# A tuned RMS-norm kernel rewritten as hardware loops with hand-made semaphores

## The chip, the cores and the metric

One NeuronCore of a Trainium2 chip runs the kernel. The metric is device time in microseconds (us) of one execution. All runs quoted are in the fast state, with a granted clock of 1.0 (TensorE's, as the profile gives it), so times can be compared directly. The profile's span is about 2 us shorter than the measured time (162.0 against 164.03 us for the kernel before).

Engine names in the profile: DVE is VectorE, ACT is ScalarE, POOL is GpSimd, SP is SyncE, which here only issues transfers. A name with q (ACTq, DVEq, SPq) is that engine's sequencer; in these profiles the waits of an engine on the hand-made semaphores are put down to it.

## The reference, cut to what matters

```python
x: (16, 1024, 512) float32; gamma: (512,) ones; eps: 1e-5
rms = np.sqrt(np.mean(x ** 2, axis=-1, keepdims=True) + eps)
return np.maximum(x / rms * gamma, 0)
```

There are 16384 rows of 512 floats, 33.55 MB in and as much out.

## The kernel before

Each of 128 partitions handles 128 rows, in eight chunks of 16 rows (4.19 MB). Six chunk buffers ("slots") are loaded at once; loads 6 and 7 reuse the first two slots when their stores are done. A chunk is computed in two groups of G = 8 rows:

```python
junk = psum.tile([P, d], F32, name="junk")            # one scratch row
...
for g in range(ngroups):                              # 2 groups a chunk
    a, b = g * G, (g + 1) * G
    for j in range(a, b):
        nc.scalar.activation(out=junk, in_=xt[:, j, :], func=ACTF.Square,
                             accum_out=ss[i][:, j:j + 1])
    nc.scalar.activation(out=rms[i][:, a:b], in_=ss[i][:, a:b],
                         func=ACTF.Sqrt, bias=eps_sb, scale=inv_d)
    nc.vector.tensor_mul(out=xt[:, a:b, :], in0=xt[:, a:b, :], in1=gammaG())
    nc.vector.reciprocal(out=rstd[i][:, a:b], in_=rms[i][:, a:b])
    for j in range(a, b):
        nc.vector.tensor_scalar(out=xt[:, j, :], in0=xt[:, j, :],
            scalar1=rstd[i][:, j:j + 1], scalar2=0.0, op0=ALU.mult, op1=ALU.max)
```

The squares themselves go to `junk` and are never read; only the row sum is used. The framework writes everything out as straight code and places all waits.

Of the kernel before, what the change touches and what calls it, by code (L numbers as in the profile page):

```python
# [1 line left out]

# [4 lines left out]

F32 = mybir.dt.float32
ALU = mybir.AluOpType
ACTF = mybir.ActivationFunctionType  # L10


@with_exitstack
def kernel(
    ctx: ExitStack,
    tc: tile.TileContext,
    x: bass.AP,
    gamma: bass.AP,
    eps: bass.AP,
    out: bass.AP,  # L20
):


    nc = tc.nc
    P = nc.NUM_PARTITIONS

    x2 = x.flatten_outer_dims()
    out2 = out.flatten_outer_dims()
    n, d = x2.shape
    rows = n // P  # L30
    inv_d = 1.0 / d
    xv = x2.rearrange("(c p k) d -> c p k d", p=P, k=16)
    ov = out2.rearrange("(c p k) d -> c p k d", p=P, k=16)

    K = 16
    G = 8
    nchunks = rows // K
    nslots = 6
    ngroups = K // G

    singles = ctx.enter_context(tc.tile_pool(name="singles", bufs=1))
    slots = ctx.enter_context(tc.tile_pool(name="slots", bufs=1))
    small = ctx.enter_context(tc.tile_pool(name="small", bufs=1))
    psum = ctx.enter_context(
        tc.tile_pool(name="psum", bufs=1, space=bass.MemoryType.PSUM))

    ctx.enter_context(tc.manual_schedule())

    gseed = singles.tile([P, d], F32, name="gseed")
    gamma_sb = singles.tile([P, d], F32, name="gamma_sb")  # L50
    eps_sb = singles.tile([P, 1], F32, name="eps_sb")
    junk = psum.tile([P, d], F32, name="junk")
    slot = [slots.tile([P, K, d], F32, name=f"slot{s}") for s in range(nslots)]
    ss = [small.tile([P, K], F32, name=f"ss{i}") for i in range(nchunks)]
    rms = [small.tile([P, K], F32, name=f"rms{i}") for i in range(nchunks)]
    rstd = [small.tile([P, K], F32, name=f"rstd{i}") for i in range(nchunks)]

    def load(i):
        nc.sync.dma_start(out=slot[i % nslots], in_=xv[i])

    def store(i):
        nc.sync.dma_start(out=ov[i], in_=slot[i % nslots])

    def gammaG():
        g = gamma_sb[:]
        return bass.AP(tensor=g.tensor, offset=g.offset,
                       ap=[g.ap[0], [0, G], g.ap[1]])

    def compute(i):
        xt = slot[i % nslots]  # L70
        for g in range(ngroups):
            a, b = g * G, (g + 1) * G
            for j in range(a, b):
                nc.scalar.activation(out=junk, in_=xt[:, j, :], func=ACTF.Square,  # L74
                                     accum_out=ss[i][:, j:j + 1])
            nc.scalar.activation(out=rms[i][:, a:b], in_=ss[i][:, a:b],  # L76
                                 func=ACTF.Sqrt, bias=eps_sb, scale=inv_d)
            nc.vector.tensor_mul(out=xt[:, a:b, :], in0=xt[:, a:b, :], in1=gammaG())  # L78
            nc.vector.reciprocal(out=rstd[i][:, a:b], in_=rms[i][:, a:b])  # L79
            for j in range(a, b):  # L80
                nc.vector.tensor_scalar(  # L81
                    out=xt[:, j, :], in0=xt[:, j, :],
                    scalar1=rstd[i][:, j:j + 1], scalar2=0.0,
                    op0=ALU.mult, op1=ALU.max)

    nc.vector.memset(gseed, 0.0)  # L86
    nc.vector.memset(eps_sb, eps)  # L87
    for q in range(0, P, 32):
        nc.scalar.dma_start(out=gseed[q:q + 1, :], in_=gamma[None, :])

    for i in range(min(nslots, nchunks)):
        load(i)
    nc.vector.stream_shuffle(gamma_sb, gseed, [0] * 32)  # L93
    for i in range(min(nslots, nchunks)):
        compute(i)
    nxt = nslots
    for i in range(nchunks):
        store(i)
        if i >= 1 and nxt < nchunks:
            load(nxt)  # L100
            compute(nxt)
            nxt += 1


# [1 line left out]
_INS = ['x', 'gamma', 'eps']  # L106
_OUTS = [((16, 1024, 512), 'float32')]

_NUMBERS = {'eps': 9.999999747378752e-06}


# [26 lines left out]
```

## Time and profile before

| quantity | value | where it is read |
|---|---|---|
| time | 164.03 us (163.9 to 164.15, 2 runs) | the timed runs |
| bytes moved | 67.11 MB on one queue, 96.9% of 16 engines' span | queue table |
| DVE busy / ACT busy | 124.6 / 98.5 us | busy table |
| a DVE group / an ACT group | 7.74 / 6.24 us | timeline |
| last store issued / span's end | 143.01 / 162.0 us | timeline |

The prediction reads the bound from the slice view. The windows view of the end shows what it means for the last store. Its columns are the window, its length, the busy time of DVE, ACT and POOL with instruction counts, the clock, the DMA share and GB/s.

```profile
140.00:147.00 7.00, 2.98 (x8) 0.00 (x0) 0.00 (x0) 1.00 1.02 440
147.00:152.00 5.00, 0.00 (x0) 0.00 (x0) 0.00 (x0) 1.00 0.99 426
152.00:157.00 5.00, 0.00 (x0) 0.00 (x0) 0.00 (x0) 1.00 1.02 439
157.00:161.00 4.00, 0.00 (x0) 0.00 (x0) 0.00 (x0) 1.00 0.27 115
```

The last store is issued when compute is finished:

```profile
143.01 0.33 SPq L62 DMA_DIRECT2D out_dram<-slot  x1
```

The queue works in the order of issue: the first four loads, issued at 0.73, 1.16, 1.64 and 2.10 us, land at 13.0, 22.8, 32.7 and 42.3.

### The profile page before, as it was taken

Reading aid. Unit: us, or ns where it says so; the run is one execution under the profiler, and the core shown is the slowest. Engines: PE = TensorE matmul, PEld = TensorE weight load, DVE = VectorE, ACT = ScalarE, POOL = GpSimd, SP = SyncE. Lnnn points to the kernel's source line nnn. Section 1 sums busy time; section 2 is a strip of 40 time slices with the busy share of each in tenths; the row PEclk is TensorE's granted clock in tenths of the full one; section 3 lists DMA queues with packets and bytes.
Section 4 is the critical chain, followed back from the end, with each engine's and each line's share of the span. In section 5 each row is a group of like instructions: output and inputs, shape, how many; then the busy total and the mean of one; then the engine's idle time right before and its main releaser. Section 6 shows DMA issues by size and latency. Waiting matters only on the chain.

```text
span 162.0 us, 554 instructions
## 1 busy us (share of the span) xinstructions
DVE 124.6 (77%) x164; ACT 98.5 (61%) x274; POOL 0.2 (0%) x4
## 2 busy tenths in 40 slices
DVE  1001299999999999999999999999999999920000
ACT  2107999999999999999999199901998000000000
POOL 0000000000000000000000000000000000000000
DMA  6999899999999999998999999999999999999990
GB/s 227 421 405 502 388 413 493 390 421 477 396 421 471 396 388 388 461 445 388 463 437 404 453 445 404 453 437 396 461 429 445 429 421 445 429 421 445 437 413 16
DMA packets 2315, 67.14 MB, mean 414 GB/s; under 512 B 260, under 2 KB 260, under 8 KB 264
## 3 DMA queue, kind: packets, MB, share of 16 engines
q1 hardware_dynamic: 2304, 67.11, 96.9%
q14 instruction: 3, 0.02, 0.0%
q10 hardware_dynamic: 8, 0.01, 0.0%
HBM read 33.56 MB, written 33.55 MB: 414 GB/s over the span
## 4 chain that ended last, share of the span: by engine, by line
DVE 74%; DMA 8%; ACT 3%; issue 2%; DVEq 0%
DVE slot L78 43%; DVE slot L81 30%; DMA slot<-in_x_dram 8%; ACT junk L74 3%; DVE rstd L79 1%; DVEq L133 0%
## 5 line engine op out<-in xcount | busy, mean ns | idle before, releaser
L74 ACT ACTIVATE junk<-slot 128x512 f32<-128x512 f32 x128 | 76.8, 600 | 23.0 <-DMA slot<-in_x_dram 19.5
L78 DVE TENSOR_TENSOR slot<-slot,gamma_sb 128x4096 f32<-128x4096 f32 x16 | 70.7, 4418 | 4.2 <-ACT junk L74 4.2
L81 DVE TENSOR_SCALAR slot<-slot,rstd 128x512 f32<-128x512 f32 x128 | 52.1, 481 | 0.6
L74 ACT ACTIVATION_READ_ACCUMULATOR junk<-slot 128x1 f32 x128 | 23.8, 186 | 0.0
L93 DVE LOAD_MASK_SELECT gamma_sb<-gseed x1 | 0.0, 14 | 12.8 <-DMA gseed<-in_gamma_dram 12.8
L76 ACT ACTIVATE rms<-ss,eps_sb 128x8 f32<-128x8 f32 x16 | 4.8, 301 | 0.5
L74 ACT ACT_TABLE_LOAD x1 | 1.3, 1283 | 3.2 <-issue 3.2
L79 DVE RECIPROCAL rstd<-rms 128x8 f32<-128x8 f32 x16 | 3.1, 194 | 0.0
L76 ACT ACT_TABLE_LOAD x1 | 1.3, 1283 | 0.0
L86 DVE MEMSET gseed<- 128x512 f32 x1 | 0.5, 485 | 0.9 <-PEq L119 0.9
L93 DVE STREAM_SHUFFLE gamma_sb<-gseed 128x512 f32<-128x512 f32 x1 | 0.7, 721 | 0.0
L119 POOL MEMSET const-bfloat16-1.0<- 128x1 bf16 x1 | 0.1, 101 | 0.0
L119 POOL MEMSET const-uint8-127<- 128x1 uint8 x1 | 0.1, 101 | 0.0
L119 POOL MEMSET const-float32-0.0<- 128x1 f32 x1 | 0.1, 99 | 0.2 <-issue 0.2
L119 POOL MEMSET const-float32-1.0<- 128x1 f32 x1 | 0.1, 98 | 0.0
L87 DVE MEMSET eps_sb<- 128x1 f32 x1 | 0.1, 59 | 0.0
## 6 DMA issues: line engine op xcount, KB each, us to landing
slot<-in_x_dram SPq DMA_DIRECT2D x8, 4096.0 KB, 30.6
out_dram<-slot SPq DMA_DIRECT2D x8, 4096.0 KB, 35.4
gseed<-in_gamma_dram ACTq DMA_DIRECT2D x4, 2.0 KB
```

Source lines behind the costliest of these rows:

```text
L74: nc.scalar.activation(out=junk, in_=xt[:, j, :], func=ACTF.Square, accum_out=ss[i][:, j:j + 1])
L76: nc.scalar.activation(out=rms[i][:, a:b], in_=ss[i][:, a:b], func=ACTF.Sqrt, bias=eps_sb, scale=inv_d)
L78: nc.vector.tensor_mul(out=xt[:, a:b, :], in0=xt[:, a:b, :], in1=gammaG())
L79: nc.vector.reciprocal(out=rstd[i][:, a:b], in_=rms[i][:, a:b])
L81: nc.vector.tensor_scalar(out=xt[:, j, :], in0=xt[:, j, :], scalar1=rstd[i][:, j:j + 1], scalar2=0.0, op0=ALU.mult, op1=ALU.max)
L86: nc.vector.memset(gseed, 0.0)
L87: nc.vector.memset(eps_sb, eps)
L93: nc.vector.stream_shuffle(gamma_sb, gseed, [0] * 32)
L119: nc = _bacc.Bacc("TRN2", target_bir_lowering=False, num_devices=1)
```

## The change

The intent is a short program: one critical section (a stretch in which the author, not the framework, places the waits) in which ACT and DVE each run a hardware loop over the 16 groups, with register addresses and the author's own semaphores. Transfers keep their order and sizes. On DVE the reciprocal, which waits for ACT's Sqrt, moves ahead of the multiply. The core of the diff:

```diff
-    junk = psum.tile([P, d], F32, name="junk")
+    junk = psum.tile([P, G, d], F32, name="junk")
+    with tc.tile_critical():
...
+        for i in range(nchunks):
+            nc.gpsimd.wait_ge(sem_ld[i], 16)
+            nc.gpsimd.sem_inc(ready, per)
...
+        with nc.scalar.Fori(0, ngroups) as gi:
+            nc.scalar.wait_ge(ready, 1)
+            nc.scalar.sem_inc(ready, -1)
+            base = nc.scalar.snap((gi % (nslots * per)) * G)
+            col = nc.scalar.snap(gi * G)
+            for j in range(G):
+                a = nc.scalar.activation(
+                    out=junk[:, j, :], in_=slots[:, bass.ds(base + j, 1), :],
+                    func=ACTF.Square, accum_out=ss[:, bass.ds(col + j, 1)])
+                if j == G - 1:
+                    a.then_inc(sa, 1)
+            nc.scalar.wait_ge(sa, 1)
+            nc.scalar.sem_inc(sa, -1)
+            nc.scalar.activation(out=rms[:, bass.ds(col, G)], in_=ss[:, bass.ds(col, G)],
+                                 func=ACTF.Sqrt, bias=eps_sb, scale=inv_d).then_inc(sq, 1)
...
+        with nc.vector.Fori(0, ngroups) as gi:
+            nc.vector.wait_ge(sq, 1)
...
+            nc.vector.reciprocal(out=rstd[:, bass.ds(col, G)], in_=rms[:, bass.ds(col, G)])
+            nc.vector.tensor_mul(out=blk, in0=blk, in1=gammaG).then_inc(sv, 1)
+            nc.vector.wait_ge(sv, 1)
+            nc.vector.sem_inc(sv, -1)
... (eight tensor_scalar, the last raising `done`)
```

More of the change, by code (lines that the diff above doesn't have):

```diff
@@ L31 @@
     inv_d = 1.0 / d
-    xv = x2.rearrange("(c p k) d -> c p k d", p=P, k=16)
-    ov = out2.rearrange("(c p k) d -> c p k d", p=P, k=16)
     K = 16
@@ L38 @@
     nslots = 6
-    ngroups = K // G
+    ngroups = rows // G
+    per = K // G
+    xv = x2.rearrange("(c p k) d -> c p k d", p=P, k=K)
+    ov = out2.rearrange("(c p k) d -> c p k d", p=P, k=K)
     singles = ctx.enter_context(tc.tile_pool(name="singles", bufs=1))
-    slots = ctx.enter_context(tc.tile_pool(name="slots", bufs=1))
-    small = ctx.enter_context(tc.tile_pool(name="small", bufs=1))
     psum = ctx.enter_context(
         tc.tile_pool(name="psum", bufs=1, space=bass.MemoryType.PSUM))
-    ctx.enter_context(tc.manual_schedule())
     gseed = singles.tile([P, d], F32, name="gseed")
@@ L51 @@
     eps_sb = singles.tile([P, 1], F32, name="eps_sb")
-    junk = psum.tile([P, d], F32, name="junk")
-    slot = [slots.tile([P, K, d], F32, name=f"slot{s}") for s in range(nslots)]
-    ss = [small.tile([P, K], F32, name=f"ss{i}") for i in range(nchunks)]
-    rms = [small.tile([P, K], F32, name=f"rms{i}") for i in range(nchunks)]
-    rstd = [small.tile([P, K], F32, name=f"rstd{i}") for i in range(nchunks)]
+    ss = singles.tile([P, rows], F32, name="ss")
+    rms = singles.tile([P, rows], F32, name="rms")
@@ new lines @@
+    rstd = singles.tile([P, rows], F32, name="rstd")
+    slots = singles.tile([P, nslots * K, d], F32, name="slots")
+    junk = psum.tile([P, G, d], F32, name="junk")
+    sem_ld = [tc.alloc_semaphore(f"ld{i}") for i in range(nchunks)]
+    sem_st = [tc.alloc_semaphore(f"st{i}") for i in range(nchunks)]
+    sem_g = tc.alloc_semaphore("gam")
+    sem_e = tc.alloc_semaphore("epsr")
+    sem_z = tc.alloc_semaphore("zero")
+    ready = tc.alloc_semaphore("ready")
+    sq = tc.alloc_semaphore("sq")
@@ L58, in load @@
+    done = tc.alloc_semaphore("done")
+    sa = tc.alloc_semaphore("sa")
+    sv = tc.alloc_semaphore("sv")
     def load(i):
-        nc.sync.dma_start(out=slot[i % nslots], in_=xv[i])
+        s = (i % nslots) * K
+        nc.sync.dma_start(out=slots[:, s:s + K, :], in_=xv[i]).then_inc(sem_ld[i], 16)
     def store(i):
-        nc.sync.dma_start(out=ov[i], in_=slot[i % nslots])
-    def gammaG():
-        g = gamma_sb[:]
-        return bass.AP(tensor=g.tensor, offset=g.offset,
-                       ap=[g.ap[0], [0, G], g.ap[1]])
@@ L69, in compute @@
-    def compute(i):
-        xt = slot[i % nslots]
-        for g in range(ngroups):
-            a, b = g * G, (g + 1) * G
-            for j in range(a, b):
-                nc.scalar.activation(out=junk, in_=xt[:, j, :], func=ACTF.Square,
-                                     accum_out=ss[i][:, j:j + 1])
-            nc.scalar.activation(out=rms[i][:, a:b], in_=ss[i][:, a:b],
-                                 func=ACTF.Sqrt, bias=eps_sb, scale=inv_d)
-            nc.vector.tensor_mul(out=xt[:, a:b, :], in0=xt[:, a:b, :], in1=gammaG())
-            nc.vector.reciprocal(out=rstd[i][:, a:b], in_=rms[i][:, a:b])
-            for j in range(a, b):
-                nc.vector.tensor_scalar(
-                    out=xt[:, j, :], in0=xt[:, j, :],
-                    scalar1=rstd[i][:, j:j + 1], scalar2=0.0,
-                    op0=ALU.mult, op1=ALU.max)
@@ L86 @@
-    nc.vector.memset(gseed, 0.0)
-    nc.vector.memset(eps_sb, eps)
-    for q in range(0, P, 32):
-        nc.scalar.dma_start(out=gseed[q:q + 1, :], in_=gamma[None, :])
-    for i in range(min(nslots, nchunks)):
-        load(i)
-    nc.vector.stream_shuffle(gamma_sb, gseed, [0] * 32)
-    for i in range(min(nslots, nchunks)):
-        compute(i)
-    nxt = nslots
-    for i in range(nchunks):
-        store(i)
-        if i >= 1 and nxt < nchunks:
-            load(nxt)
-            compute(nxt)
-            nxt += 1
+        s = (i % nslots) * K
@@ new lines, in store @@
+        nc.sync.dma_start(out=ov[i], in_=slots[:, s:s + K, :]).then_inc(sem_st[i], 16)
+    g = gamma_sb[:]
+    gammaG = bass.AP(tensor=g.tensor, offset=g.offset,
+                     ap=[g.ap[0], [0, G], g.ap[1]])
+    with tc.tile_critical():
+        for i in range(min(nslots, nchunks)):
+            load(i)
+        nxt = nslots
+        for i in range(nchunks):
+            nc.sync.wait_ge(done, per * (i + 1))
+            store(i)
+            if i >= 1 and nxt < nchunks:
+                nc.sync.wait_ge(sem_st[nxt - nslots], 16)
+                load(nxt)
+                nxt += 1
+        for i in range(nchunks):
+            nc.sync.wait_ge(sem_st[i], 16)
+        for i in range(nchunks):
+            nc.gpsimd.wait_ge(sem_ld[i], 16)
+            nc.gpsimd.sem_inc(ready, per)
+        nc.vector.memset(gseed, 0.0).then_inc(sem_z, 1)
+        nc.vector.memset(eps_sb, eps).then_inc(sem_e, 1)
+        nc.scalar.wait_ge(sem_z, 1)
+        for q in range(0, P, 32):
+            nc.scalar.dma_start(out=gseed[q:q + 1, :],
+                                in_=gamma[None, :]).then_inc(sem_g, 16)
+        nc.scalar.wait_ge(sem_e, 1)
+        with nc.scalar.Fori(0, ngroups) as gi:
[13 more added lines that the diff above has]
+                                 func=ACTF.Sqrt, bias=eps_sb, scale=inv_d).then_inc(sq, 1)
+        nc.vector.wait_ge(sem_g, 64)
+        nc.vector.stream_shuffle(gamma_sb, gseed, [0] * 32).then_inc(sv, 1)
+        nc.vector.wait_ge(sv, 1)
+        nc.vector.sem_inc(sv, -1)
+        with nc.vector.Fori(0, ngroups) as gi:
+            nc.vector.wait_ge(sq, 1)
+            nc.vector.sem_inc(sq, -1)
+            base = nc.vector.snap((gi % (nslots * per)) * G)
+            col = nc.vector.snap(gi * G)
+            blk = slots[:, bass.ds(base, G), :]
+            nc.vector.reciprocal(out=rstd[:, bass.ds(col, G)], in_=rms[:, bass.ds(col, G)])
+            nc.vector.tensor_mul(out=blk, in0=blk, in1=gammaG).then_inc(sv, 1)
+            nc.vector.wait_ge(sv, 1)
+            nc.vector.sem_inc(sv, -1)
+            for j in range(G):
+                row = slots[:, bass.ds(base + j, 1), :]
+                r = nc.vector.tensor_scalar(
+                    out=row, in0=row,
+                    scalar1=rstd[:, bass.ds(col + j, 1)], scalar2=0.0,
+                    op0=ALU.mult, op1=ALU.max)
+                if j == G - 1:
+                    r.then_inc(done, 1)
```

## The prediction

> **What bounds the kernel now.** I read the slice view first, because it says at once whether an engine or the DMA is never idle. Each digit is the busy share, in tenths, of one fortieth of the 162.0 us span.
>
> ```profile
> DVE  1001299999999999999999999999999999920000
> ACT  2107999999999999999999199901998000000000
> ...
> DMA  6999899999999999998999999999999999999990
> GB/s 227 421 405 502 388 413 493 390 421 477 396 421 471 396 388 388 461 445 388 463 437 404 453 445 404 453 437 396 461 429 445 429 421 445 429 421 445 437 413 16
> ```
>
> The DMA row is full from the first slice to the last but one; VectorE (DVE) fills only the middle and ScalarE (ACT) less. The queue table agrees: one queue carries everything and takes 96.9% of sixteen engines' span.
>
> ```profile
> q1 hardware_dynamic: 2304, 67.11, 96.9%
> ```
>
> So the bound is the traffic: 67.11 MB between about 1.7 us (first bytes) and 158.1 us (last bytes), 156.4 us, is 429 GB/s, and one 4.19 MB chunk takes 9.8 us. The page's chain of waits nevertheless names DVE for 74%. It follows the last store back to the instruction that allowed it, without asking whether the store then had to queue. So I looked at how much slack compute has. The timeline gives the last store's issue as 143.01 us; the sixteen transfers of 9.8 us run in issue order, so its own bytes start only at 148.4 us. DVE is about 5 us early. That slack is what the change can spend before the time moves.
>
> Next, the pace of the two engines, from the timeline around the first group:
>
> ```profile
> 18.33 0.60 ACT L74 ACTIVATE junk<-slot 128x512 f32<-128x512 f32 x1
> 18.87 0.19 ACT L74 ACTIVATION_READ_ACCUMULATOR junk<-slot 128x1 f32 x1
> 19.07 1.28 ACT L76 ACT_TABLE_LOAD   x1
> ...
> 20.37 0.30 ACT L76 ACTIVATE rms<-ss,eps_sb 128x8 f32<-128x8 f32 x1
> 20.57 0.58 ACT L74 ACTIVATE junk<-slot 128x512 f32<-128x512 f32 x1
> ```
>
> Starts are what count here. Squares start 0.755 us apart (17.58, 18.33 in the same timeline), the table load holds ACT from 19.07 to 20.37 (1.30 us), the sqrt occupies 0.20 us before the next square starts. Hence an ACT group of 8 rows costs 8 x 0.755 + 0.20 = 6.24 us. And, decisively, there are only two table loads in the whole program, one for the first Square and one for the first Sqrt:
>
> ```profile
> L74 ACT ACT_TABLE_LOAD x1 | 1.3, 1283 | 3.2 <-issue 3.2
> L76 ACT ACT_TABLE_LOAD x1 | 1.3, 1283 | 0.0
> ```
>
> After the second load the Squares run without another. DVE's group, from the chain: 4.33 (the multiply by gamma) + 0.12 (reciprocal) + 0.02 + 3.26 (eight row scalings, 0.407 apart) = 7.74 us, and 16 of them from 19.09 end at 142.9. DVE is the slower engine by 1.5 us a group, both are ahead of the DMA.
>
> [...]sqrt starts 1.30 us after the load starts, and the load starts 0.01 us after the accumulator read ends. I use 1.30. [...]
>
> **The change, part by part.** I read the built program, engine by engine.
>
> *Table loads.* [...] The loop body holds two loads[...]. The same program position that cost two loads in all now costs 2 x 16 = 32. Thirty more at 1.30 us are 39 us on ACT. They sit in ACT's own order, between a wait for data and the squares, and between the squares and the sqrt, so nothing on ACT hides them.
>
> *Own wait before the sqrt.* ACT now waits for its last accumulator, takes the count down, does a register add and then issues the load: I estimate 0.2 us a group.
>
> *Registers and loop.* Each row gets two register instructions on its engine. On ACT they have 0.755 us to run in[...], so I count nothing. The loop's branch and the next group's address work fall under the 1.3 + 0.3 us of load and sqrt; nothing again. On DVE each row has only 0.407 us, so there the register work may show: I allow 0.02 to 0.1 us a row.
>
> So ACT's group is 1.30 + 6.04 + 0.20 + 1.30 + 0.30 = 9.14 us against 6.24.
>
> *DVE.* Reciprocal moves ahead of the multiply, so the whole DVE group now waits for the sqrt, and a wait for the multiply's completion is added (about 0.2). Its group becomes some 4.33 + 0.12 + 0.3 + 3.3 to 4.1 = 8.1 to 8.9 us. That is under 9.14, so DVE follows ACT and idles between groups.
>
> *Instructions removed, GpSimd relay.* The program is shorter, but no trace line shows instruction supply limiting anything, so that gains nothing. Load completion passes through GpSimd to ACT: about 0.2 us, once, on the path.
>
> *Does the DMA still cover this?* No. ACT at 9.14 us for half a chunk is 18.3 us a chunk, while the DMA needs 2 x 9.8 = 19.6 us for a chunk's load and store. In steady state the DMA would still be slower. But the loads of six chunks go out first, in 60 us, and compute starts at 13 us. At the end only stores are left, and these go at 9.8 us each while compute produces one every 18.3. The first stores go out in time: chunk 4's is issued at 13.4 + 10 x 9.14 + 8.3 = 113 us against its slot at 119. Chunk 5 is ready at 131.4, but its slot begins at 128.9, so there the DMA runs dry, and stays so for chunks 6 and 7.
>
> *The path that sets the end, then:*
> - first chunk at ACT: 13.06 in the trace, plus relay, wait and addresses 0.35: 13.4
> - 16 ACT groups x 9.14 = 146.2: last sqrt done at 159.6
> - last DVE group, nothing overlapping it: 8.2 to 8.9, say 8.5: 168.1
> - last store, alone: first bytes 0.9 us after issue (0.73 to about 1.7 for the first load), 9.8 us of bytes, and 2.8 us from last bytes to completion (158.1 to 160.97, as the store queue's last wait says): 13.5, so 181.6
> - end of the program: 1.0 us as before (160.97 to 162.0), plus 0.6 estimated for the critical section's own closing barrier: 183.2
> - measured time is 164.03 for a span of 162.0, so 2.0 more: 185.2.
>
> I put the point at 186, for the register work is more likely dearer than free.
>
> **The rivals.**
> 1. *DVE becomes the bound.* For it: 0.407 us a row leaves little room for two register instructions and a dispatch with register addresses, and nothing in this profile prices them. Against: [...]the row may be 0.5 us before DVE reaches ACT's 9.14. At 0.6 us a row DVE's group is 4.33 + 0.12 + 0.3 + 4.8 = 9.55, and the time is 13.4 + 9.14 + 16 x 9.55 + 13.5 + 1.6 + 2.0 = 192 us.
> 2. [...]
> 3. *The transfers hide it.* If the loads in the loop were cheap when repeated, ACT's group would be 6.24 + 0.2 + 0.1, DVE at 8.1 would set the pace, start at about 22, and end at 151.6; with 13.5, 1.6 and 2.0 that is 169. Even then the 5 us of slack is spent. Only with both free tables and free registers would it stay within 2%. For this the profile offers only that the DMA is full now.
> 4. *Faster.* Would need less traffic or an earlier first byte; traffic is unchanged and the first load is issued after one more branch. Nothing speaks for it.
>
> **Range and chances.** The certain part is 30 loads of 1.28 us on an engine with no slack behind it. An error of 0.1 us in the group's time is worth 1.6 us in the result. Low end: no wait cost on ACT, DVE tail 8.0, giving about 181; I take 180. High end: rival 1[...], 203. Faster by over 2%: 1%. Within 2%: 4%. Slower: 95%.
>
> **What would show it.** In the profile after: 32 table loads, 16 on each of the two lines, at about 1283 ns, ACT busy near 98.5 + 38.5 = 137 us; DMA digits full until about 129 us and then gaps; ACT group starts 9.1 us apart; DVE idle before its reciprocal, released by ACT; the last store issued near 168 us. Wrong if there are fewer loads, if ACT waits for transfers after the first chunk, if DVE is never idle between groups (rival 1)[...].

## More of the kernel before

The DMA goes on at full rate (426 to 440 GB/s) to about 158 us. The 115 GB/s of the last window are an average: 393 in its first microsecond, then single late packets (33 GB/s in each of the next two).

## The result, and the profile after

The changed kernel takes 166.1 us (166.07 to 166.14, 2 runs) against 164.03. Ratios in this document are the mean time of one kernel's fast runs over that of the other's of the same rounds, so not quite the ratio of the medians quoted; here it is 1.0127, with a 95% interval of 1.0083 to 1.017. The prediction was 186 us, at least 180. The kernel is slower by about 2 us, where 22 had been forecast; the prediction gave a time within 2% of the kernel before a chance of 4%.

The slice view of the changed kernel, same rows as before:

```profile
DVE  1001069999999999999999999999999999998000
ACT  0006999999999999999999999999999999800000
...
DMA  6999999999999999999999999999999999992892
GB/s 200 440 401 472 407 439 455 392 455 431 415 471 392 455 312 471 423 415 471 392 439 455 392 455 415 439 439 415 447 431 423 447 415 423 463 407 120 384 511 128
```

ACT is busy from the fourth slice on and full from the fifth almost to the end; before, it had gaps in the second half. The DMA row has one hole, in the 37th slice (120 GB/s). It was predicted to run dry from about 129 us; it does so only at about 148.5. The windows view of that stretch, to be held against the one of before:

```profile
140.00:147.00 7.00, 6.84 (x10) 2.97 (x8) 0.00 (x0) 1.00 1.02 440
147.00:152.00 5.00, 4.29 (x9) 0.00 (x0) 0.00 (x0) 1.00 0.31 131
152.00:157.00 5.00, 0.00 (x0) 0.00 (x0) 0.00 (x0) 1.00 0.98 419
157.00:161.00 4.00, 0.00 (x0) 0.00 (x0) 0.00 (x0) 1.00 1.22 524
```

DVE is still working in the window in which the DMA starves. The DMA waits for the last store, issued at 151.48 us instead of 143.01:

```profile
151.48 0.33 SPq L72 DMA_DIRECT2D out_dram<-slots  x1
```

Then the groups, for the table loads and for the instruction that waits for ACT (busy, mean ns, idle before and its releaser):

```profile
L110 ACT ACT_TABLE_LOAD x16 | 20.5, 1283 | 14.0 <-ACTq L106 13.7
L117 ACT ACT_TABLE_LOAD x16 | 20.5, 1283 | 2.7 <-ACTq L116 2.7
L130 DVE RECIPROCAL rstd<-rms x16 | 3.2, 203 | 7.8 <-DVEq L126 6.9
```

Sixteen and sixteen, 1283 ns each: the 32 table loads are there as predicted. So the cost was real, and something else must have become cheaper. The timeline of the first group shows it; the columns are start, length, engine and line, operation, and the idle time before it:

```profile
13.73 1.28 ACT L110 ACT_TABLE_LOAD   x1 [13.73 <-ACTq L106]
...
15.03 0.60 ACT L110 ACTIVATE junk<-slots 128x512 f32 x1
15.56 0.19 ACT L110 ACTIVATION_READ_ACCUMULATOR junk<-slots  x1
15.65 0.58 ACT L110 ACTIVATE junk<-slots 128x512 f32 x1
...
20.20 1.28 ACT L117 ACT_TABLE_LOAD   x1 [0.17 <-ACTq L116]
21.50 0.30 ACT L117 ACTIVATE rms<-ss,eps_sb  x1
21.81 1.28 ACT L110 ACT_TABLE_LOAD   x1
```

The same stretch of the kernel before:

```profile
17.58 0.60 ACT L74 ACTIVATE junk<-slot 128x512 f32<-128x512 f32 x1
18.12 0.19 ACT L74 ACTIVATION_READ_ACCUMULATOR junk<-slot 128x1 f32 x1
18.33 0.60 ACT L74 ACTIVATE junk<-slot 128x512 f32<-128x512 f32 x1
```

A Square now starts about 0.1 us before the accumulator read of the one before it has ended (15.65 against 15.56 + 0.19). Starts are 0.61 us apart. In the kernel before, the next Square started 0.02 us after the read, and starts were 0.755 us apart. The ACT group is 21.81 - 13.73 = 8.08 us, not 9.14.

DVE is tied to ACT all the way to the end. Two late groups:

```profile
134.76 0.30 ACT L117 ACTIVATE rms<-ss,eps_sb  x1
...
135.32 0.20 DVE L130 RECIPROCAL rstd<-rms  x1
...
142.85 0.30 ACT L117 ACTIVATE rms<-ss,eps_sb  x1
...
143.42 0.20 DVE L130 RECIPROCAL rstd<-rms  x1
```

Each reciprocal starts 0.26 to 0.27 us after the end of its Sqrt, much as the first one did (0.25) at 22.05, when DVE had stood idle (21.50 + 0.30 = 21.80). If DVE were the slower of the two, this lag would grow from group to group. The group table can mislead here. It shows hardly any idle time before the reciprocal after the first one, because the wait happens to end just as DVE's previous rows do (132.00 + 3.26 = 135.26, and the reciprocal starts at 135.32).

So where did the 2 us come from? The last store goes out 8.5 us later: DVE starts 22.05 - 19.09 = 3.0 us later, since it now waits for two table loads and the Sqrt, and its 16 groups are 8.09 - 7.74 = 0.35 us longer each, 5.6 us in all. Most of these 8.5 us are absorbed. In the kernel before the last store had to queue until about 148.4 us anyway, so only 3.1 us are left. From there it took 12.6 us to complete (at 160.97), because of the late packets (33 GB/s from 158 to 160 us); the changed kernel's last store, which has the engines to itself after the pause, moves 524 GB/s in the last window and takes 11.1 us (to 162.58). That leaves 1.6 us. The end of the program, 1.4 us instead of 1.0, makes it 2.

### The profile page after: what moved, and what is told of

It is laid out like the page before. It is cut to its first block, busy times and chain, and to the rows that moved or that the text cites. A ratio compares the mean times of both kernels' runs of the same rounds, so it can differ in the third digit from the quotient of the medians.

```text
span 164.0 us, 1246 instructions
## 1 busy us (share of the span) xinstructions
DVE 127.2 (78%) x164; ACT 126.1 (77%) x304; POOL 0.2 (0%) x4
## 5 line engine op out<-in xcount | busy, mean ns | idle before, releaser
L110 ACT ACTIVATE junk<-slots 128x512 f32 x128 | 74.3, 580 | 0.2
L131 DVE TENSOR_TENSOR slots<-slots,gamma_sb 128x4096 f32 x16 | 70.8, 4426 | 0.0
L136 DVE TENSOR_SCALAR slots<-slots,rstd x128 | 52.1, 482 | 2.5 <-DVEq L133 2.5
L110 ACT ACT_TABLE_LOAD x16 | 20.5, 1283 | 14.0 <-ACTq L106 13.7
L110 ACT ACTIVATION_READ_ACCUMULATOR junk<-slots x128 | 23.8, 186 | 0.0
L117 ACT ACT_TABLE_LOAD x16 | 20.5, 1283 | 2.7 <-ACTq L116 2.7
L130 DVE RECIPROCAL rstd<-rms x16 | 3.2, 203 | 7.8 <-DVEq L126 6.9
L117 ACT ACTIVATE rms<-ss,eps_sb x16 | 4.8, 301 | 0.2
```

Source lines behind the costliest of these rows:

```text
L110: a = nc.scalar.activation(out=junk[:, j, :], in_=slots[:, bass.ds(base + j, 1), :], func=ACTF.Square, accum_out=ss[:, bass.ds(col + j, 1)])
L117: nc.scalar.activation(out=rms[:, bass.ds(col, G)], in_=ss[:, bass.ds(col, G)], func=ACTF.Sqrt, bias=eps_sb, scale=inv_d).then_inc(sq, 1)
L130: nc.vector.reciprocal(out=rstd[:, bass.ds(col, G)], in_=rms[:, bass.ds(col, G)])
L131: nc.vector.tensor_mul(out=blk, in0=blk, in1=gammaG).then_inc(sv, 1)
L136: r = nc.vector.tensor_scalar(out=row, in0=row, scalar1=rstd[:, bass.ds(col + j, 1)], scalar2=0.0, op0=ALU.mult, op1=ALU.max)
```

## The experiments

My theory, A, has three parts. The Squares got faster because they no longer wait for each other, which hid most of the price of the table loads. ACT at 8.09 us a group sets DVE's pace. The DMA sets the end as soon as the last store is ready by about 149 us. The rivals are named with each run. Each kernel was timed beside the kernel before on the same chip in three rounds: its median was 164.31 us beside the first four, 164.36 beside the last three. All results were correct. The changed kernel was not timed again in these rounds, so a comparison of a run with its 166.1 us is one across rounds.

### e1_row_wait: put the wait back

```diff
-                if j == G - 1:
-                    a.then_inc(sa, 1)
-            nc.scalar.wait_ge(sa, 1)
-            nc.scalar.sem_inc(sa, -1)
+                a.then_inc(sa, 1)
+                if j < G - 1:
+                    nc.scalar.wait_ge(sa, j + 1)
+            nc.scalar.wait_ge(sa, G)
+            nc.scalar.sem_inc(sa, -G)
```

> The changed kernel with one thing put back: each Square waits for the one before it (own count, taken down once a group). Theory A (the prediction failed because the Squares of the changed kernel no longer wait for each other, 0.61 us apart instead of 0.755): Squares go back to 0.755 us apart or more, as the register work of a row now lies behind the wait; ACT group 9.1 to 10.5 us, time 182 to 205 us; with exactly 0.755 the recorded sum comes out at about 183. Rival B (the eight PSUM banks, not the missing wait, made the Squares faster): they stay near 0.61 us apart and the time near 166.

Measured: 202.25 us, ratio 1.2312 (1.2282 to 1.2343). The timeline:

```profile
47.05 0.60 ACT L110 ACTIVATE junk<-slots 128x512 f32 x1 [0.21 <-ACT junk L110]
47.59 0.19 ACT L110 ACTIVATION_READ_ACCUMULATOR junk<-slots  x1
47.99 0.60 ACT L110 ACTIVATE junk<-slots 128x512 f32 x1 [0.21 <-ACT junk L110]
```

Squares are 0.935 us apart, with 0.21 us of idle time that the profile puts down to the Square before. All eight rows of `junk` (the "banks") are still in use, so rival B falls. The ACT group is 10.35 us (table loads at 44.82 and 55.17), which is 8.08 plus seven times 0.325. The missing waits were worth 36 us in this kernel, counting the register work that they uncover (see e6). It also shows that the path of the prediction, from ACT's pace to the end, was right: 13.73 + 16 x 10.35 for the groups, 8.3 for the last DVE group, 11.1 for a lone store as in the changed kernel, and 1.4 + 2.1 for the end, make 202.2.

### e2_before_banks: take the wait out of the kernel before

```diff
-    junk = psum.tile([P, d], F32, name="junk")
+    junk = [psum.tile([P, d], F32, name=f"junk{b}") for b in range(G)]
...
-                nc.scalar.activation(out=junk, in_=xt[:, j, :], func=ACTF.Square,
+                nc.scalar.activation(out=junk[j % G], in_=xt[:, j, :], func=ACTF.Square,
```

> The kernel before with eight scratch tiles for the squares instead of one, nothing else; its built program has no wait of a Square on a Square any more. Theory A: Squares 0.61 us apart, ACT busy down or the same, an ACT group 5.1 to 5.3 us instead of 6.24, but the time stays at 164.0 within 0.5 us, because DVE (7.74 us a group) and the DMA set it. Rival C (Squares are faster only in the loop, by register addressing or another form of instruction): 0.755 us apart as before.

Measured: 164.11 us, ratio 0.998 (0.9952 to 1.0009). From its timeline:

```profile
30.10 0.58 ACT L74 ACTIVATE junk<-slot 128x512 f32<-128x512 f32 x1
30.62 0.19 ACT L74 ACTIVATION_READ_ACCUMULATOR junk<-slot 128x1 f32 x1
30.71 0.58 ACT L74 ACTIVATE junk<-slot 128x512 f32<-128x512 f32 x1
```

Squares start 0.61 us apart in straight code with fixed addresses, so rival C falls. An ACT group is 5.23 us (30.10 to 35.33) instead of 6.24, ACT is busy for 86.1 us instead of 98.5, and the time does not move. After the first group nothing waits for ACT here.

### e3_one_table: one table load a group

```diff
+    scrap = singles.tile([P, 1], F32, name="scrap")
...
+            nc.scalar.activation(out=scrap, in_=eps_sb, func=ACTF.Sqrt)
             nc.scalar.wait_ge(ready, 1)
```

> The changed kernel with a one-element Sqrt at the head of ACT's loop, ahead of its wait for data, so the head loads the table that holds both functions: one load a group instead of two. Theory A (ACT at 8.09 us a group sets DVE's pace in the changed kernel, DVE's own need being 8.03): ACT group about 7.0 us, DVE starts near 19.4 us, its groups 8.03 us apart, no longer tied to ACT, and ends near 148; the last store then queues behind the one before, and the time is 163.8 to 164.8 us. Rival D (the 2 us are the cost of the critical section itself, of barriers and the relay over GpSimd): the time stays at 165.7 to 166.4.

Measured: 163.68 us, ratio 0.9959 (0.9933 to 0.9984), just under the range that I had given. ACT's group is 6.91 us (Sqrt at 18.83 and 25.73). The page has 16 table loads (L106, 1283 ns each) instead of 32, none at the lines of the Squares and of the group's Sqrt (L112, L119), and the results are correct, so one load serves both functions here. DVE at its own pace:

```profile
121.13 0.20 DVE L132 RECIPROCAL rstd<-rms  x1
...
128.94 0.20 DVE L132 RECIPROCAL rstd<-rms  x1
...
136.76 0.20 DVE L132 RECIPROCAL rstd<-rms  x1
```

That is 7.81 us a group, not the 8.03 that I had read out of the changed kernel; a reciprocal that need not wait starts 0.08 us before the last row has ended and lets the multiply follow after 0.11 instead of 0.19 us. So ACT did set the pace, by 0.28 us a group. DVE ends at 144.7 and the whole 2 us are gone, with loop, relay over GpSimd and critical section all still in place. Rival D falls.

### e4_mul_first: multiply ahead of the reciprocal

```diff
             nc.scalar.sem_inc(sa, -1)
+            nc.scalar.sem_inc(sd, 1)
...
-            nc.vector.wait_ge(sq, 1)
+            nc.vector.wait_ge(sd, 1)
...
-            nc.vector.reciprocal(...)
-            nc.vector.tensor_mul(out=blk, in0=blk, in1=gammaG).then_inc(sv, 1)
+            nc.vector.tensor_mul(out=blk, in0=blk, in1=gammaG)
+            nc.vector.wait_ge(sq, 1)
+            nc.vector.sem_inc(sq, -1)
+            nc.vector.reciprocal(...).then_inc(sv, 1)
```

> The changed kernel with the multiply by gamma ahead of the reciprocal again, released by the Squares instead of the Sqrt; the reciprocal waits for the Sqrt. Two table loads a group stay. Theory A: DVE starts at about 20.1 instead of 22.05 us, its groups stay 8.09 us apart (ACT's pace), it ends at about 149.6, the last store goes out 1.9 us earlier, the time is 164.2 to 165.2. Rival E (the added wait in the middle of DVE's group costs more than the earlier start gives): DVE's groups are 8.2 us or more apart and the time is 166 or more.

Measured: 165.53 us, ratio 1.0074 (1.0049 to 1.0099). Neither expectation held. DVE starts 1.5 us earlier, at 20.52, but the groups are 8.16 us apart (multiplies at 28.69 and 36.85). The extra time is on ACT: the idle time before the Sqrt's table load is 0.24 us instead of 0.17, the price of my own additional count; e7, which has it too, shows the same step against e3 (0.26 instead of 0.19 us). Sixteen times 0.07 is 1.1 us, so the last store goes out at 150.92 instead of 151.48. In both traces the queue waits 10.5 us for its completion after issuing it (11.1 us from the start of the issue to landing in the changed kernel), so the end follows the last store one to one. The medians differ by 0.57 us (166.10 to 165.53), but the intervals of the two ratios overlap, so the times alone do not show this gain.

### e5_unrolled: no hardware loops

```diff
-        with nc.scalar.Fori(0, ngroups) as gi:
+        for gi in range(ngroups):
...
-        with nc.vector.Fori(0, ngroups) as gi:
+        for gi in range(ngroups):
... (fixed indices in place of the registers)
```

> The changed kernel with both hardware loops written out (same counts, same order, same eight banks, fixed addresses); the built program then has two table loads in all. Theory A: ACT group about 5.5 us, DVE starts near 21.7 us, its groups about 7.82 us apart as in the run with one table load, its end near 147, before the store in front of the last one has left the DMA (about 149), so the time is at the transfers' floor: 163.4 to 164.4 us. Rival F (the register work of the loop also cost time beside the table loads): DVE's group falls clearly under 7.8 us, to 7.6 or less.

Measured: 165.06 us (164.82 to 165.18), ratio 1.0037 (1.002 to 1.0054), 0.4 us over the range at its nearest. The compute side is as expected: two table loads, an ACT group of 5.3 us, and DVE groups of 7.81 us (131.02 to 138.83). That is the same as with the loop in e3, so two register instructions a row cost DVE nothing, and rival F falls. The last store goes out at 146.76, earlier than in e6, but the time is higher. What differs is the transfers. The trace shows 33 GB/s in each of the three microseconds from 158 to 161, single late packets, where e3 has none after 159. The queue's own waits show that the lag arises before the last transfer: after issuing the last store (until 147.09 us in e5, 145.02 in e3) the queue waits 5.0 and 5.6 us for the fifteenth transfer, so until about 152.1 and 150.6, and then 9.6 us for the last one in both. I have no shown cause for that, and it stays open. It is also a warning: at the floor of the transfers, differences of half a microsecond in this kernel can't be put down to compute.

### e6_unrolled_row_wait: the wait alone

The edit of e1 applied to e5.

> The written-out kernel, in which each Square waits for the one before it, still with eight banks. Theory A: the wait alone makes Squares 0.755 us apart (against 0.61), with no register work behind it, so the 0.935 of the run with a wait in the loop is 0.755 plus about 0.18 of address work that the wait uncovers. ACT group about 6.6 us; time still 163.4 to 164.6 us. Rival B (banks): 0.61 to 0.7 us apart.

Measured: 164.25 us (163.85 to 165.19), ratio 1.0005 (0.9966 to 1.0045).

```profile
14.74 0.60 ACT L110 ACTIVATE junk<-slots 128x512 f32<-128x512 f32 x1
15.27 0.19 ACT L110 ACTIVATION_READ_ACCUMULATOR junk<-slots 128x1 f32 x1
15.49 0.60 ACT L110 ACTIVATE junk<-slots 128x512 f32<-128x512 f32 x1
```

Squares are 0.755 us apart, to the hundredth the spacing of the kernel before, with eight rows of `junk` and fixed addresses. A wait on the Square before costs 0.14 us a row (0.755 against 0.61 in e5). The ACT group is 6.32 us, where I had expected 6.6. In e1, with register addresses, a row costs 0.18 us more (0.935 against 0.755). I read this as address work that stands behind the wait instead of running ahead of it; that it stems from the loop is shown, where it sits is not.

The fourth cell of this square, one scratch row and no wait, was not run. So whether a shared scratch row alone would also slow the Squares is not shown; it isn't needed to explain the numbers.

### e7_one_table_mul_first: both mends of the loop

> Both mends of the loop at once: one table load a group and the multiply ahead of the reciprocal. Theory A: DVE starts near 19.1 us, is tied to nothing, groups 7.8 to 8.0 us apart, ends near 145 to 147, under the 149 at which the DMA can take the last store: 163.4 to 164.4 us, no faster than one table load alone, since the transfers set the end. A rival that still sees compute on the path expects another 0.5 us or more below 163.7.

Measured: 164.0 us, ratio 0.9973 (0.9957 to 0.999). DVE starts at 19.09, is never held by ACT again, and issues the last store at 144.91; the time is that of the transfers, as theory A has it. With e3 it is the best version, both a few tenths of a per cent under the kernel before, well inside what counts as the same. No run got below 163.4 us.

## Why the prediction was wrong

**The bound and the slack: right.** The kernel before waits for the DMA, and compute can lose several microseconds without effect. e2, e3, e6 and e7, whose last stores go out anywhere from 142.1 to 147.7 us, have medians between 163.7 and 164.3 us. The exception is e5 (146.76 us, 165.06), whose transfers lagged for a reason that is open.

**Table loads: right.** There were 32, at 1.30 us each from start to next start (13.73 to 15.03, 20.20 to 21.50), with no idle time after them: a load is 1.28 us long and the next instruction starts 0.02 us after its end. ACT was busy for 126.1 us, not the 137 forecast, because Squares without a wait overlap; in e2 that alone took ACT's busy time from 98.5 to 86.1 us.

**The step that failed is the 6.04 (8 x 0.755) in "1.30 + 6.04 + 0.20 + 1.30 + 0.30 = 9.14 us", carried over from the kernel before.** Squares and own wait, 6.04 + 0.20, measured 5.17 us (15.03 to 20.20), of which the own wait is 0.17; the other terms measured 1.30, 1.30 and 0.31. I took the spacing of the Squares for the price of the instruction, when 0.14 us of it was a wait that this very change removes. The evidence was there before the run: the timeline has a Square start 0.02 us after the accumulator read of the one before ends, the built program carries a wait on nearly every Square, and the diff gives `junk` eight rows. I even wrote that the removed instructions gain nothing, and none of my rivals lets a Square become cheaper. In the steady state the group is 8.09 us, so the term is worth 16 x 1.05 = 16.8 us.

**A second step was right only because the first was wrong.** The prediction let ACT's register work run free within the 0.755 us of a row. It is free in the changed kernel, where no Square waits for another: rows are 0.61 us apart there and in e5, which has no register work, and the next group's table load starts 0.01 us after the Sqrt's end (21.81 against 21.50 + 0.30). With the wait that the 0.755 contains, e1 shows 0.935 us a row and 202 us, not 186.

**Smaller terms.** The lone last store took 11.1 us from issue to landing, not 13.5: the 2.8 us from last bytes to completion that I took from the kernel before were late packets, not a fixed delay. DVE's last group took 8.3 instead of 8.5 us, the end 1.4 instead of 1.6, the start 13.73 instead of 13.4, and the difference of time and span 2.1 instead of 2.0. With all these, 185.2 - 16.8 + 0.3 - 0.2 - 2.4 - 0.2 + 0.1 = 166.0, against 166.1 measured. On top of the sum I had added 0.8 us for register work on DVE; e3 against e5 shows that it is free (7.81 us a group in both). The prices of waits and barriers were estimates of mine that no trace of the kernel before could show: 0.2 us for ACT's own wait (measured 0.17), 0.2 for DVE's (0.16 us of idle time before the rows), 0.35 from the first chunk's landing to ACT's first work (13.37 to 13.73, 0.36), 0.6 more at the program's end (0.4).

**Where the DMA runs dry: off by 20 us**, for the same reason. With 8.09 us a group, chunk 6 is stored at 135.29, before its turn, and only chunk 7 comes late.

**Rivals.** Rival 3 put 169 us on a kernel in which DVE at 8.1 us sets the pace from about 22 us on. That is nearly the arithmetic of what happened, but for another reason: the loads were not cheap, ACT still set the pace, and the lone store was 2.4 us shorter than I thought. Rival 1 fell: DVE's rows start 0.396 us apart in the traces of both kernels. (The prediction's 0.407 is 3.26 / 8, the length of a whole stretch over its rows; and by its own terms DVE would have reached 9.14 us at 0.55 us a row, not 0.5.) The high end of 203 us was my estimate; the sum of rival 1 gives 192, and no number of this case gives the rest.

## What to carry to other kernels

The spacing of equal instructions in a trace can be instruction plus wait (here 0.755 us was 0.61 plus 0.14); before carrying it over to a changed kernel, ask for each gap which wait makes it and whether the change removes that wait. A scratch output that nobody reads can still slow an engine, through the waits that keep its writes in order (here 0.755 against 0.61 us a row): rotate it. Look at the function tables in every loop body too, where a load that was paid once may be paid in each turn (here 2 loads became 32, and 2 again when the loop was written out in e5). And before valuing any of this, find out how late the last transfer could have been issued, for only what goes beyond that point reaches the time (here 148.4 us, where the store was issued at 143.01).
